# Products of constants ahead of the low-rank and the scaled keys' products in one half of a preparation

## The chip, the cores and the metric

The kernel runs on one core of a Trainium2 chip. A core has five engines with a queue each: TensorE (PE, with its weight loads shown apart as PEld), VectorE (DVE), ScalarE (ACT), GpSimd (POOL) and SyncE (SP, which issues the loads here). The metric is device time in microseconds, the median of several runs. TensorE runs at one of two granted clocks, 2.4 or 1.2 GHz; the profile writes them as 1.00 and 0.50.

## The reference, cut to what matters

One layer over 256 latent tokens with 256 context tokens ahead of them, in float32:

```python
z_x, z_c = split_cols(h_x @ w_in), split_cols(h_c @ w_in)
# RWKV-7 branch, per direction d: context scan, then the latent scan from its final state
wl = w0 + einsum('btzr,zrc->btzc', tanh(lw), w_lora_b)      # low-rank, two directions
decay = exp(-exp(-softplus(-wl) - 0.5))
a = sigmoid(a0 + einsum('btzr,zrc->btzc', la, a_lora_b))
s = s * w_t - (s @ kk_t) (kk_t * a_t)^T + v_t k_t^T         # one step of a scan
# neighbourhood attention beside it, branch merge, output projection
# mixture of 16 experts, top 2, added to the residual
```

## The kernel before, in words

The program is emitted once, straight through, and a list scheduler then orders each engine's queue from dependencies and its own costs; on each queue the order is fixed from then on. Weights come through a ring of three buffers (`wraw`, 512 KB each): a load is issued when the buffer's last user is done.

The scans are done in chunks of 32 tokens. `rw_prep(s, R)` prepares a stream (s = 0 context, s = 1 latent) in two halves f of four heads each, for two directions d: `low_rank(f)` (products into `p2`, `tanh` on ACT, L680), `decays(f, d)` (scan along tokens on DVE, L693; exponentials on ACT, L694 and L695; scaled keys on DVE and POOL, L705 to L710), `products(f, d)` (64 x 64 products of the scaled keys into `pp`, evacuated by DVE, L733, and ACT, L736) and `turn` (transposes). Then `rw_solve` inverts the chunks' triangles on DVE (L785 to L795), and `rw_chain` runs the chunks one after the other. Every matmul is issued at L264 (`mm`), except transposes (L749, L967) and the products of constants (L275).

Between the steps `fill()` pulls steps of a second program, `others()`: projections, attention (`att_core`: logits in `pa`, softmax at L999 to L1005, transposes of the probabilities at L967) and the modulation's rows (`mod_part`, weights `in_modr`, 32 x 256 products into `pb`). In the latent preparation the attention's second group of heads and the modulation stand beside it, and the second half f = 1 begins once the attention is emitted.

`warm(p, site, n)` issues as many products of two constants as the table `WARM` gives for the site, bfloat16, 128 x 128 by n columns, into the PSUM tile p that the products behind it overwrite. Nothing reads them. Each is ordered behind the last matmul of the main program that was emitted before it. Before the change the table has sites in the second half of the latent chain ("x", "y", "z") and behind it ("gn").

Of the kernel before, what the change touches and what calls it, by code (L numbers as in the profile page):

```python
# [168 lines left out]

WARM = {(w, 1, i): n for w, n in (("x", 4), ("y", 3), ("z", 2)) for i in range(3, 8)}  # L170
WARM.update({("gn", i): n for i, n in enumerate((4, 4, 10, 3, 5, 5))})
MIX = [3, 1]
DEEP = [3]

# [58 lines left out]
def hybrid_kernel(ctx: ExitStack, tc: tile.TileContext, a, out, dbg=None, stop=None):  # L233
# [23 lines left out]
    def pb(name="pb"):  # L257
        return ps.tile([128, 512], F32, tag="b", name=name, bufs=4)
# [312 lines left out]
    p, p2 = fout["lw"]  # L571
# [89 lines left out]
    def rw_prep(s, R):  # L661
# [6 lines left out]
        def low_rank(f):  # L668
            for i, (b, src, o) in enumerate(((wlb, lw, 0), (alb, la, 8))):
                p2 = [pb(), pb()]  # L670
                for q in range(2):
                    for d in range(2):
                        r_ = slice(64 * d, 64 * d + 64)
                        Q = 2 * f + q
                        mm(p2[d][:, q * 256:(q + 1) * 256], b[r_, Q * 128:(Q + 1) * 128], src[r_, t_])
                fill()
                for d in range(2):
                    for q in range(2):
                        Q = 2 * f + q
                        S.activation(tmps[d][i][:, q * 256:(q + 1) * 256], p2[d][:, q * 256:(q + 1) * 256], AF.Tanh, scale=0.5,  # L680
                                     bias=hb[:, o + 4 * d + Q:o + 4 * d + Q + 1])
# [31 lines left out]
        def products(f, d):  # L713
            bk, Gd = tmps[d][3], GG[f][d]
            mG = C[f"maskG{d}"]

            w = 32 * nw
            pp = [pb(), pb()]
            for i in range(8):
                if i and i % 2 == 0:  # L720
                    fill()
                for par in range(2):
                    j = 2 * i + par
                    for h in range(2):
                        r_ = slice(64 * h, 64 * h + 64)
                        o_ = 64 - 64 * (h ^ par)
                        mm(pp[par][o_:o_ + 64, i * w:(i + 1) * w], bk[r_, j].rearrange("p w t -> p (w t)"),
                           Gd[r_, h, j // 8, j % 8].rearrange("p w t -> p (w t)"))
            for par in range(2):
                for h in range(2):  # L730
                    ro, o_ = 64 - 64 * h, 64 - 64 * (h ^ par)
                    pv = pp[par][:, 0:8 * w].rearrange("p (c x) -> p c x", x=w)
                    V.tensor_tensor(Gd[ro:ro + 64, h].rearrange("p q c w t -> p (q c) (w t)")[:, par::2], pv[o_:o_ + 64],  # L733
                                    mG[o_:o_ + 64, 0:w].unsqueeze(1).to_broadcast([64, 8, w]), op=ALU.mult)

                    S.activation(NT[ro + 32 * d:ro + 32 * d + 32, :, 2 * f:2 * f + 2].rearrange("p t q c -> p (q c) t")[:, par::2],  # L736
                                 pv[o_ + 32 * d:o_ + 32 * d + 32, :, 0:32], AF.Copy, scale=-1.0)
            tot = 32 if d == 0 else 1
            G.tensor_tensor(bk.ap.rearrange("p c w t -> p c (w t)"), bk.ap.rearrange("p c w t -> p c (w t)"),
                            Es[d][:, :, tot:tot + 1].to_broadcast([128, 16, 64]), op=ALU.mult)  # L740
# [322 lines left out]
    def others():  # L1063
        yield from values()
        done.add("v")
        yield from att_proj(0)
        yield from both_(att_core(0), att_proj(1), MIX[0])
        yield from receptances()
# [167 lines left out]
    for n4 in range(4):  # L1236
        pp = [pa()[:, :256] for _ in range(2)]
# [270 lines left out]
```

## Time and profile before

| | |
|---|---|
| runs, us | 737.54, 741.64, 742.75 (median 741.64) |
| the profiled execution | 737.73 us |
| its span, first to last instruction | 735.9 us |
| mean granted TensorE clock | 0.97 |
| busy share: PE, DVE, ACT, POOL | 93%, 54%, 41%, 14% |

The profile is of one execution. Times in it count from its first instruction. The latent preparation lies at about 255 to 334 us, the latent solve at 334 to 376, the latent chain up to 438, and the experts from 502 on.

### The profile page before, as it was taken

The page shows a single profiled execution, that of the slowest core. Times are in us where ns is not written, and L with a number is a line of the kernel's source. Part 1 is how long each engine was busy: PE and PEld are TensorE (multiplying, and loading weights), DVE is VectorE, ACT ScalarE, POOL GpSimd, SP SyncE. Part 2 cuts the span into 40 slices and gives each one's busy share as a digit, 9 for nine tenths or more (in the row PEclk, how much of TensorE's full clock was granted, in tenths as well). Part 3 has the DMA queues.
Part 4 walks back from the last instruction along what each step waited for, and adds up shares of the span by engine and source line. Part 5 has one row for each costly group of instructions (what it writes and reads, how often), then busy time and mean ns, then how long its engine had stood idle before and what let it go on. Part 6 is the DMA issues. An engine that isn't in the chain of part 4 may idle for free.

```text
span 735.9 us, 14592 instructions
## 1 busy us (share of the span) xinstructions
PE 681.6 (93%) x6053; PEld 455.6 (62%) x6059; DVE 397.4 (54%) x738; ACT 301.4 (41%) x604; POOL 101.0 (14%) x90
## 2 busy tenths in 40 slices
PE   4999788999999979689999998998999999999996
PEld 2667677885777844367988766995534544544532
DVE  2445985999774586968975456844213212212113
ACT  5436677447755366845444423432201101101110
POOL 0002354003223044350012201000000000000000
PEclk9999879999999977999999999999999999999999
DMA  9844011231120343777651158969999999999951
GB/s 363 324 168 134 4 59 37 80 107 59 59 63 20 112 147 113 237 262 261 201 193 60 56 197 306 361 245 381 410 408 411 409 410 412 406 411 411 409 220 61
DMA packets 46297, 165.34 MB, mean 225 GB/s; under 512 B 5392, under 2 KB 6800, under 8 KB 45328
## 3 DMA queue, kind: packets, MB, share of 16 engines
q1 hardware_dynamic: 46224, 164.34, 59.9%
q8 instruction: 49, 0.80, 0.4%
q14 instruction: 24, 0.20, 0.1%
HBM read 163.27 MB, written 1.05 MB: 223 GB/s over the span
## 4 chain that ended last, share of the span: by engine, by line
PE 73%; DVE 12%; ACT 9%; issue 2%; DMA 2%; POOL 1%; DVEq 0%; ACTq 0%; POOLq 0%
PE pa L264 53%; PE pb L264 16%; DVE arena_q L281 3%; ACT arena L753 2%; ACT arena L736 1%; PE pb L275 1%; PE pa L967 1%; ACT arena_q L280 1%; DVE arena L696 1%; DVE arena L790 1%; DVE arena L792 1%; DMA arena<-in_modr_dram 1%; DMA arena<-in_pab_dram 1%; DVE arena L693 1%; PE pb L338 1%
## 5 line engine op out<-in xcount | busy, mean ns | idle before, releaser
L264 PE MATMUL pa<-arena_p,arena_q 128*128 128x256 f32 (+1 forms) x984 | 164.3, 314 | 3.3 <-ACT arena_p L373 1.2
L264 PEld LDWEIGHTS pa<-arena_p,arena_q 128*128 128x128 f32 x984 | 134.5, 189 | 24.1 <-issue 5.5
L264 PE MATMUL pa<-arena,arena_m 128*64 128x512 f32 (+1 forms) x652 | 147.1, 555 | 0.0
L264 PE MATMUL pb<-arena 128*32 128x64 f32 (+13 forms) x2248 | 112.0, 270 | 17.7 <-DVE arena L710 5.7
L264 PEld LDWEIGHTS pb<-arena 128*32 128x32 f32 (+7 forms) x2246 | 70.3, 137 | 54.7 <-issue 19.7
L264 PEld LDWEIGHTS pa<-arena,arena_m 128*64 128x64 f32 x652 | 48.5, 137 | 83.7 <-issue 80.3
L280 ACT CAST arena_q<-arena 128x1024 fp32r<-128x1024 f32 (+1 forms) x66 | 62.8, 955 | 80.9 <-PE pa L264 55.1
L281 DVE TENSOR_TENSOR arena_q<-arena,arena_q 128x1024 fp32r<-128x1024 f32 (+1 forms) x66 | 77.6, 1176 | 23.3 <-ACT arena_q L280 18.7
L1408 DVE TENSOR_TENSOR arena_m<-arena_m,pa 128x512 f32<-128x512 f32 x8 | 5.5, 688 | 96.7 <-PE pa L264 96.7
L264 PE MATMUL pa<-arena_q,arena_p 128*128 128x256 f32 x384 | 57.2, 296 | 0.0
L264 PEld LDWEIGHTS pa<-arena_q,arena_p 128*128 128x128 f32 x384 | 49.4, 194 | 6.3 <-issue 3.6
L813 POOL TENSOR_TENSOR arena<-arena 64x512 f32<-64x512 f32 x30 | 32.0, 1068 | 115.6 <-DVE arena L843 113.7
L1349 ACT ACTIVATE arena_m<-pa,arena 128x128 f32<-128x128 f32 x32 | 12.1, 457 | 78.0 <-PE pa L264 78.0
L264 PE MATMUL pa<-arena_p,arena_m 128*64 128x512 f32 x140 | 41.3, 593 | 0.0
L264 PE MATMUL pa<-arena 128*64 128x256 f32 (+5 forms) x192 | 37.8, 446 | 1.7 <-ACT arena L968 1.7
L280 ACT CAST arena_r<-arena_m 128x512 fp32r<-128x512 f32 x16 | 9.9, 618 | 64.9 <-DVE arena_m L1428 64.9
L1428 DVE SCALAR_TENSOR_TENSOR arena_m<-pa,arena,arena_p 128x512 f32<-128x512 f32 x16 | 12.0, 751 | 43.1 <-PE pa L264 43.1
L264 PEld LDWEIGHTS pa<-arena_m,arena 128*128 128x128 f32 x256 | 30.8, 201 | 6.6 <-issue 5.7
L809 ACT COPY arena<-arena 32x256 f32<-32x256 f32 x64 | 25.8, 403 | 18.7 <-PE pb L264 16.8
L264 PE MATMUL pa<-arena_m,arena 128*128 128x128 f32 x256 | 32.3, 287 | 0.9 <-DVE arena_m L1336 0.9
L843 DVE TENSOR_TENSOR arena<-pb,arena 64x512 f32<-64x512 f32 x30 | 20.7, 689 | 15.9 <-PE pb L264 15.4
L264 PE MATMUL pb<-arena,arena 64*64 64x64 f32 (+1 forms) x496 | 26.9, 251 | 0.7 <-ACT arena L829 0.6
(210 smaller groups left out, 846.2 us busy)
## 6 DMA issues: line engine op xcount, KB each, us to landing
arena<-in_w_dram SPq DMA_DIRECT2D x137, 512.0 KB, 9.6
arena<-in_win_dram SPq DMA_DIRECT2D x42, 512.0 KB, 4.0
arena_p<-in_w_dram SPq DMA_DIRECT2D x35, 512.0 KB, 10.1
arena<-in_modr_dram SPq DMA_DIRECT2D x32, 512.0 KB, 4.1
arena<-in_modw_dram SPq DMA_DIRECT2D x4, 2048.0 KB, 14.3
arena<-in_w_dram SPq DMA_DIRECT2D x20, 256.0 KB, 8.2
arena_m<-in_w_dram SPq DMA_DIRECT2D x10, 512.0 KB, 8.8
arena<-in_pab_dram SPq DMA_DIRECT2D x8, 512.0 KB, 3.2
```

The costliest lines, as they stand in the source:

```text
L264: i = T.matmul(out, lhsT, rhs, start=start, stop=stop, skip_group_check=True)
L275: i = T.matmul(p[:, 512 - n:], cb("ob", 128), cb("scanm", n), start=True, stop=True, skip_group_check=True)
L280: S.copy(dhi.bitcast(F32R), src)
L281: eng.tensor_tensor(dlo.bitcast(F32R), src, dhi, op=ALU.subtract)
L338: T.transpose(p[:, (2 * k + i) * 128:(2 * k + i + 1) * 128], xn[:, 2 * st + i, kc * 128:(kc + 1) * 128], ident)
L693: V.tensor_tensor_scan(cum[:, go], C["scanm"], sg[:, go], 0.0, op0=ALU.mult, op1=ALU.add)
L753: (V.tensor_copy if h and c2 else S.copy)(BT[f][64 - 64 * h:128 - 64 * h, d, q, c2:8:2, :], pv[64 * c2:64 * c2 + 64, :, h, :])
L809: S.copy(Z[rv, h, :, d, :], vt[32 * c4:32 * c4 + 32, h, tt, :, :])
L813: G.tensor_tensor(sd[r_], Z[r_, h], pc[r_, :, :, i].rearrange("p d q -> p q d").unsqueeze(3) .to_broadcast([64, 4, 2, 64]), op=ALU.mult)
L843: V.tensor_tensor(Z1[r_, h], pyv[r_], sd[r_], op=ALU.add)
L1349: S.activation(dst, src, AF.Identity, scale=m4[:, kc:kc + 1], bias=m3[:, kc:kc + 1])
L1428: V.scalar_tensor_tensor(sil.ap, py[n2], gsl[pr % 2].ap, m5r[:, n2 * 512:(n2 + 1) * 512], op0=ALU.mult, op1=ALU.mult)
```

## The change

Two sites are added to the table, each with a call: three products of 512 columns ahead of each of the two parts of `low_rank(0)` of the latent stream, and six of 256 columns ahead of `products(0, d)` for each direction. These are 18 products, 6,144 columns in all. The second half (f = 1) and the context's preparation have none.

```diff
 WARM.update({("gn", i): n for i, n in enumerate((4, 4, 10, 3, 5, 5))})
+WARM.update({("low", 1, 0, i): 3 for i in range(2)})
+WARM.update({("prod", 1, 0, d): 6 for d in range(2)})
...
         def low_rank(f):
             for i, (b, src, o) in enumerate(((wlb, lw, 0), (alb, la, 8))):
                 p2 = [pb(), pb()]
+                warm(p2[i], ("low", s, f, i))
...
             w = 32 * nw
             pp = [pb(), pb()]
+            warm(pp[0], ("prod", s, f, d), 256)
             for i in range(8):
```

The scheduler then orders all queues anew from this place to the solve. Line numbers behind the new lines are larger by 2 to 4 (L264 becomes L266, L275 becomes L277, L693 becomes L696, L705 becomes L708, L999 becomes L1003, L967 becomes L971).

TensorE at the latent low-rank, before: the low-rank products are the rows of 128x256, the attention's logits those of pa 128x512, the modulation's those of 32x256.

```order
L264 MATMUL pb<-arena 128x512 x2
L264 MATMUL pb<-arena 128x256 x6
L264 MATMUL pa<-arena 128x512 x2
L264 MATMUL pb<-arena 128x256 x2
L264 MATMUL pb<-arena 32x256 x8
```

TensorE there, after the change, from the third of the first three products of constants:

```order
L277 MATMUL pb<-arena 128x512
L266 MATMUL pb<-arena 128x256 x4
L277 LDWEIGHTS arena
L277 MATMUL pb<-arena 128x512
L277 LDWEIGHTS arena
L277 MATMUL pb<-arena 128x512
L277 LDWEIGHTS arena
L277 MATMUL pb<-arena 128x512
L266 MATMUL pb<-arena 128x256 x2
L266 MATMUL pa<-arena 128x512
L266 MATMUL pb<-arena 128x256 x2
L266 MATMUL pa<-arena 128x512
```

Six products of constants stand ahead of low-rank products, and the second low-rank part now alternates with the logits.

TensorE ahead of the first `products(0, 0)` (the row of 64x64), before:

```order
L264 MATMUL pa<-arena 128x512 x2
L264 MATMUL pb<-arena 32x256 x4
L967 MATMUL pa<-arena 128x128 x4
L264 MATMUL pb<-arena 32x256 x4
L967 MATMUL pa<-arena 128x128 x4
L264 MATMUL pb<-arena 32x256 x4
L264 MATMUL pa<-arena 128x512
L264 MATMUL pb<-arena 64x64 x32
```

TensorE there, after the change, from the last of the six products of constants:

```order
L277 LDWEIGHTS arena
L277 MATMUL pb<-arena 128x256
L266 MATMUL pb<-arena 32x256 x8
L971 MATMUL pa<-arena 128x128 x4
L266 MATMUL pb<-arena 64x64 x24
L266 MATMUL pb<-arena 32x256 x4
L266 MATMUL pb<-arena 64x64 x8
L266 MATMUL pb<-arena 128x256 x2
L971 MATMUL pa<-arena 128x128 x4
```

The six stand ahead of two units of the modulation and four transposes of probabilities, not directly ahead of the 64x64 products; these have moved ahead of the second four transposes and of two logits.

VectorE at the beginning of `decays(0, 0)`, before (L692, L693, L696, L705 and L707 are the decays, L999 to L1005 the attention's softmax):

```order
L1115 TENSOR_TENSOR arena<-arena,pb 128x512 x2
L999 SCALAR_TENSOR_TENSOR arena<-pa,arena 128x256
L692 TENSOR_SCALAR arena<-arena 128x512 x2
L1002 TENSOR_REDUCE arena<-arena 128x1
L999 SCALAR_TENSOR_TENSOR arena<-pa,arena 128x256
L693 SCALAR_TENSOR_TENSOR arena<-arena 128x512
L696 SCALAR_TENSOR_TENSOR arena<-arena 128x512
L1004 RECIPROCAL arena<-arena 128x1
L1002 TENSOR_REDUCE arena<-arena 128x1
L1005 TENSOR_SCALAR arena<-arena 128x512
L705 TENSOR_TENSOR arena<-arena 64x16x32
L707 TENSOR_TENSOR arena<-arena 64x16x32
```

VectorE there, after the change (L695, L696, L699, L708 and L710 are the decays, L1003 to L1009 the softmax):

```order
L1119 TENSOR_TENSOR arena<-arena,pb 128x512 x2
L695 TENSOR_SCALAR arena<-arena 128x512
L696 SCALAR_TENSOR_TENSOR arena<-arena 128x512
L1003 SCALAR_TENSOR_TENSOR arena<-pa,arena 128x256
L695 TENSOR_SCALAR arena<-arena 128x512
L708 TENSOR_TENSOR arena<-arena 64x16x32
L1006 TENSOR_REDUCE arena<-arena 128x1
L1003 SCALAR_TENSOR_TENSOR arena<-pa,arena 128x256
L699 SCALAR_TENSOR_TENSOR arena<-arena 128x512
L710 TENSOR_TENSOR arena<-arena 64x16x32
L1008 RECIPROCAL arena<-arena 128x1
L1006 TENSOR_REDUCE arena<-arena 128x1
```

The decays' scan has moved ahead of both logits' steps, and the softmax's first normalisation (L1005, now L1009) behind the two scaled keys' steps.

## Rows read from the trace of the kernel before

**Rows 1.** Part 2 of the page: granted TensorE clock, 40 slices of 18.4 us, in tenths.

```profile
PEclk9999879999999977999999999999999999999999
```

**Rows 2.** Windows of 5 us: busy us (instructions) by engine, granted clock, DMA share, GB/s.

```profile
core 0: us, PE busy (x) PEld busy (x) DVE busy (x) ACT busy (x) POOL busy (x), PEclk, DMA share, GB/s
255.00:260.00 5.00, 5.00 (x27) 3.19 (x24) 2.00 (x5) 2.86 (x6) 0.00 (x0) 1.00 0.29 105
260.00:265.00 5.00, 3.03 (x30) 0.88 (x28) 4.89 (x10) 4.46 (x11) 0.99 (x1) 1.00 0.59 207
265.00:270.00 5.00, 2.86 (x16) 1.63 (x16) 5.00 (x8) 2.55 (x6) 3.75 (x4) 0.50 0.53 193
270.00:275.00 5.00, 5.00 (x76) 2.43 (x74) 5.00 (x10) 3.87 (x8) 2.17 (x1) 0.50 0.38 127
275.00:280.00 5.00, 5.00 (x26) 2.26 (x19) 0.46 (x1) 1.54 (x4) 4.94 (x5) 0.50 0.13 36
280.00:285.00 5.00, 5.00 (x23) 2.87 (x23) 4.10 (x8) 2.72 (x6) 0.40 (x1) 0.50 0.35 116
...
295.00:300.00 5.00, 2.66 (x24) 1.63 (x24) 4.53 (x8) 4.80 (x11) 1.28 (x1) 1.00 0.56 193
```

**Rows 3.** Timeline, TensorE, 265 to 287 us: start, length, what, idle before it.

```profile
265.62 1.09 PE L967 MATMUL pa<-arena 128*128 128x128 f32 x4 [2.60 <-DVE arena L1005]
...
269.24 1.09 PE L967 MATMUL pa<-arena 128*128 128x128 f32 x4 [1.52 <-DVE arena L1005]
...
273.27 5.00 PE L264 MATMUL pb<-arena 64*64 64x64 f32 x76
...
280.07 2.92 PE L264 MATMUL pb<-arena 64*128 64x256 f32 x12
...
284.39 2.40 PE L264 MATMUL pb<-arena 64*128 64x256 f32 x28
```

**Rows 4.** Timeline, all engines, 258 to 287 us: the decays, their inputs, their products.

```profile
258.17 1.57 ACT L680 ACTIVATE arena<-pb,arena 128x256 f32<-128x256 f32 x4 [1.87 <-PE pb L264]
...
260.30 0.75 DVE L692 TENSOR_SCALAR arena<-arena 128x512 f32<-128x512 f32 x2
...
261.95 1.21 DVE L693 TENSOR_TENSOR_SCAN arena<-arena 128x512 f32<-128x512 f32 x1
...
264.01 1.18 POOL L705 TENSOR_TENSOR arena<-arena 64x512 f32<-64x512 f32 x1 [25.27 <-ACT arena L694]
...
269.62 0.68 DVE L710 TENSOR_TENSOR arena<-arena 128x512 f32<-128x512 f32 x1
...
272.83 3.02 POOL L705 TENSOR_TENSOR arena<-arena 64x512 f32<-64x512 f32 x1 [4.02 <-ACT arena L694]
...
280.43 0.69 DVE L710 TENSOR_TENSOR arena<-arena 128x512 f32<-128x512 f32 x1 [4.97 <-POOL arena L709]
...
285.99 0.66 PEld L264 LDWEIGHTS pb<-arena 64*64 64x64 f32 x20 [0.33 <-ACT arena L736]
```

**Rows 5.** Groups by line and form, 380 to 450 us: the products of constants there.

```profile
L275 PE MATMUL pb<-arena 128*128 128x256 bf16 x52 | 7.8, 275 | 0.0
L275 PE MATMUL pb<-arena 128*128 128x512 bf16 x24 | 7.5, 381 | 0.8 <-DVE arena L1173 0.5
```

**Rows 6.** Timeline, 300 to 335 us: full clock, a load's wait, the solve's start.

```profile
323.86 0.91 PE L264 MATMUL pb<-arena 64*64 64x64 f32 x32
...
326.70 0.64 PE L264 MATMUL pb<-arena 128*32 128x256 f32 x8 [1.02 <-DMA arena<-in_modr_dram]
...
333.82 1.25 DVE L785 STREAM_TRANSPOSE arena<-arena 128x1024 f32<-128x1024 f32 x1
```

**Rows 7.** Windows by stage, columns as in rows 2: the latent solve, the experts.

```profile
335.00:375.00 40.00, 38.81 (x348) 36.12 (x346) 35.96 (x82) 17.95 (x31) 0.00 (x0) 1.00 0.70 222
...
502.00:706.00 204.00, 203.27 (x1107) 96.22 (x1109) 47.63 (x114) 31.26 (x72) 0.00 (x0) 0.99 1.03 410
```

**Rows 8.** Windows of 5 us in the context's preparation, columns as in rows 2.

```profile
85.00:90.00 5.00, 0.48 (x12) 0.31 (x13) 5.00 (x6) 2.96 (x5) 2.67 (x2) 0.76 0.00 0
```

## The prediction

> **What bounds the kernel now.** Begin with the strip of the granted clock [rows 1]: it falls in two places, slices 5 to 6 (the context's preparation) and slices 15 to 16. The second is the latent preparation, and the windows of 5 us [rows 2] show it: 1.00 up to 265, 0.50 from there to 285, four windows in all. Read TensorE's busy time beside the clock. Before the fall it has 3.03 of 5 us of work, with a hole of 2.60 us that a softmax step ends [rows 3]. In the next window it has 2.86 of 5, and from 270 on it is busy 5.00 of 5, at half speed. VectorE is the opposite: 4.89, 5.00 and 5.00 up to 275, then 0.46 of 5 from 275 to 280. So first TensorE starves behind VectorE, the clock falls, and then everybody waits for a slow TensorE.
>
> What that costs is seen by holding the moment at which an input is ready against the moment at which TensorE reaches it [rows 4]. The last scaled keys of direction 0 are written at 269.62 + 0.68 = 270.30; their products begin at 273.27, since transposes, modulation and logits stand ahead on the queue at half speed. Those of direction 1 are ready at 280.43 + 0.69 = 281.12; their weights are first loaded at 285.99. The price of half speed itself: 64x64 products take 5.00 us for 76 records (66 ns each) against 0.91 for 32 (28 ns) at full clock [rows 3, 6].
>
> What a microsecond here is worth: the solve begins at 333.82 [rows 6] and fills VectorE for 35.96 of 40 us, TensorE for 38.81 [rows 7]. Behind it come the chain and the experts, where the loads run at 1.03 of their share and 410 GB/s for 204 us [rows 7]. Nothing there has slack that waits for a clock time, so I let a shift of the solve's start reach the end in full.
>
> **The change part by part.**
>
> *The products themselves.* By the groups of those that exist [rows 5], 7.5/24 = 0.31 us for 512 columns and 7.8/52 = 0.15 for 256, tails included; by columns at 2.4 GHz, 0.21 and 0.11. So 18 cost between 6 x 0.21 + 12 x 0.11 = 2.6 and 6 x 0.31 + 12 x 0.15 = 3.7 us of TensorE, and the six of direction 1 cost 1.3 instead of 0.65 if the clock is low then. On the path lie the first three, 0.64 to 0.93: they stand directly ahead of the first low-rank products, where TensorE is busy 5.00 of 5 [rows 2], and the first `tanh` at 258.17 [rows 4] waits for those. I take 0.65. The next three delay the second low-rank part as much again, but that is read one scan later. The six ahead of `products(0, 0)` fall into the hole at 263 to 265.6 and cost nothing as long as the hole is there; if the clock is kept and the hole is gone, they cost 0.65.
>
> *The new order of VectorE.* Before, the scan of direction 0 starts at 261.95, though its input step L692 started at 260.30 and takes 0.75 for two [rows 4]; a softmax step and the second L692 stood between. Now it follows directly on its first L692, which waits for two of four `tanh` (half of 1.57) from 258.17 + 0.65: ready at 259.6, scan at about 260.0. That is 1.9 us earlier with the products' delay counted, and the first POOL step of the decays (264.01) moves with it. This gain needs no clock.
>
> *The new order of TensorE.* `products(0, 0)` no longer queue behind the second transposes and two logits. If they start as soon as their input is there, that is 3.0 us earlier than 273.27 even at an unchanged 270.30, and up to 1.9 more with the scan. The other side of this is that the softmax's first normalisation goes behind two scaled keys' steps, so the transposes that ended the hole of 2.60 us come later, not earlier, by about one step of 0.7 to 1.2 us.
>
> *The clock.* The six products put 0.65 us of dense work into a hole of 2.6 us; the hole's end moves out by about the same. What TensorE does around 264 to 269 is then hardly denser than before, so I do not expect the clock to be held through. That much work does not decide it alone is also seen elsewhere: from 295 to 300 TensorE has 2.66 of 5 us and the clock stays at 1.00 [rows 2]; in the context's preparation it has 0.48 of 5 and the clock falls [rows 8]. What I do expect is a later fall, and an earlier return, because the 64x64 products start sooner and six dense products stand directly ahead of those of direction 1.
>
> *The sum.* From the start of `products(0, 0)` to that of direction 1 TensorE works without a hole from 273.27 to 285.99, 12.7 us at half clock. Moved forward by 3.0 and with 1.3 us of products at half clock put in, direction 1 starts at 284.3: a gain of 1.7 at least from the order alone. At full clock the 12.7 become 6.4, and the start is then set by its input: 281.12 less 1.9 for the scan, 279.2, a gain of 6.8. With the low clock over for the second half of that stretch, 284.3 less 3.2 is 281.1, a gain of 4.9. Of this I take off 0.9 for VectorE, which is busy 4.53 of 5 from 295 [rows 2] and passes not all of it on: 4.0 us. The profiled execution, 737.73 (a span of 735.9 and 1.8 around it), would become 733.7. It is the quick one of the runs: their median is 741.64, 3.9 above. I lay the gain to the median and say **737.6 us**.
>
> One rule of the skill speaks against a larger gain. The step that makes direction 1 late is POOL's scaled keys at 272.83, which took 3.02 us where the same step took 1.18 at 264.01 [rows 4]. The Trainium skill, SBUF — State Buffer, "SBUF: two separate sides", says that VectorE and GpSimd share one pair of ports, that whichever starts first holds it for its whole instruction and that the other waits. By that rule no clock of TensorE shortens the 3.02; by the row alone a quieter VectorE could give back 1.8, and the sum would be nearer 731.9. In the new order the same VectorE steps stand beside it, so I keep 3.02.
>
> **The rivals.**
>
> *Held through.* The clock stays at 1.00 in the whole preparation. For it: work from 263 on comes denser, and near a hole of 2.6 us a little may decide. Against it: the hole's end moves out. Direction 1 then starts at 279.2, 6.8 us earlier, and its products and those of the low rank behind it run at 28 ns instead of 66 where they still did not: 6 to 10 us in all, 732 to 735.6.
>
> *Given back by the loads.* The second half is paced not by these steps but by the modulation's weights: at 326.70 TensorE waits 1.02 us for a load [rows 6], and there are three buffers. Then products may start early and the solve still begins near 334. For it: the wait; against it: a load is issued when a product frees its buffer, so loads move with the products, and DMA is busy only 0.13 to 0.38 of the time from 270 to 285 [rows 2]. Time: 740 to 742.5.
>
> *Slower.* One mechanism: the products delay both low-rank parts by 0.65 and 1.3 us, the postponed normalisation widens the hole, the clock falls as before and stays low as long, and the six products of direction 1 cost 1.3 us at half speed on the path. It decides if the low stretch is again 20 us or more and begins no later than about 267. Price: 1.3 + 1.3, plus up to 3 for a softmax chain that ends later and holds the transposes: 744 to 747.
>
> *Not what it says.* The products might stand where TensorE is busy anyhow. The order shows that for the first six of 512 columns: they go into a stretch that was solid. If the six of 256 are also early, only their cost of 2.6 to 3.7 is left, less the order's gain: this ends within the two cases before it.
>
> **How the numbers follow.** Chances: the forecast 0.47 (735.5 to 740), held through 0.25 (731 to 735.5), given back by the loads 0.18, slower 0.10. The runs of before spread over 5.2 us, so each case is as wide again as a run's own noise. The range leaves out 2 in 10: from **731.5** (the lower half of held through lies about there) to **744** (the point where the slower case begins). One per cent of 741.64 is 7.4 us, about what a measurement of this kernel tells from no change: faster than 734.2 takes most of held through and the edge of the forecast, 0.26; slower than 749.1 is only the far end of the last case, 0.04; the rest, 0.70, is within it.
>
> **What would show it.** In the profile of the changed kernel: the scan of direction 0 (now L696) at about 260 instead of 261.95; the first 64x64 products at 269 to 270.5 instead of 273.27; the granted clock falling once, after 266, and back by about 282; the 64x64 products of direction 1 beginning at 279 to 283; the solve's transposition (now L789) at about 329.8. The prediction is wrong if the first 64x64 products are not earlier than 272, if the clock's low stretch is as long as before, or if the solve starts 4 us earlier and the end does not follow.

## The result and the profile after

The changed kernel takes 745.61 us (median of 20 runs, 739.17 to 747.88), the kernel before 738.94 in the same rounds (20 runs, 735.21 to 744.65). The ratio is **1.0062, 95% interval 1.0040 to 1.0083**: by it some 4.6 us slower, by the two medians 6.7. The forecast was 737.6 and faster; 745.61 lies above its range. Ratios leave out executions that lie more than 1.5% above a kernel's quickest.

The strip of the granted clock of the profiled execution after (745.72 us, a span of 743.8), 40 slices of 18.6 us:

```profile
PEclk9999879999999886889999999999999999999999
```

Where the strip of before has one fall from slice 15 on [rows 1], this one is low over slices 14 to 18. Slice 14 is a low stretch of 6.8 us between 235 and 250, ahead of the place of the change. The windows of 5 us, columns as in rows 2, resolve the others:

```profile
260.00:265.00 5.00, 4.95 (x34) 2.60 (x37) 2.90 (x6) 2.75 (x7) 0.00 (x0) 1.00 0.20 81
265.00:270.00 5.00, 3.79 (x42) 1.31 (x34) 4.95 (x9) 4.03 (x11) 4.57 (x4) 1.00 0.64 208
270.00:275.00 5.00, 3.51 (x77) 2.30 (x78) 5.00 (x9) 2.69 (x6) 1.11 (x2) 0.79 0.62 215
275.00:280.00 5.00, 5.00 (x15) 2.83 (x15) 1.97 (x4) 3.14 (x8) 4.94 (x4) 0.50 0.34 105
280.00:285.00 5.00, 3.76 (x10) 0.72 (x9) 2.93 (x6) 1.82 (x4) 1.97 (x2) 0.50 0.30 105
285.00:290.00 5.00, 4.84 (x10) 2.51 (x10) 3.69 (x8) 3.26 (x8) 0.00 (x0) 0.50 0.01 3
290.00:295.00 5.00, 5.00 (x75) 3.05 (x74) 4.29 (x9) 3.40 (x8) 1.48 (x3) 0.66 0.08 15
...
305.00:310.00 5.00, 3.06 (x29) 1.75 (x25) 4.13 (x9) 4.59 (x12) 0.74 (x2) 1.00 0.86 265
310.00:315.00 5.00, 3.61 (x23) 1.49 (x23) 4.14 (x6) 2.88 (x8) 2.03 (x2) 0.55 0.62 227
315.00:320.00 5.00, 5.00 (x20) 2.67 (x19) 1.19 (x3) 1.45 (x3) 2.00 (x2) 0.50 0.41 138
320.00:325.00 5.00, 5.00 (x64) 3.25 (x63) 3.77 (x5) 0.89 (x2) 4.84 (x4) 0.93 0.71 224
```

A window at 0.79 holds (1 - 0.79) x 2 x 5 = 2.1 us at half clock, one at 0.66 holds 3.4. So the first low stretch is 2.1 + 15 + 3.4 = 20.5 us, about as long as before [rows 2]; it only begins later. And there is a **second fall**: 4.5 + 5 + 0.7 = 10.2 us from 310 on, a place where the prediction did not look.

To compare executions whose earlier parts differ (this one is 3.2 us late already when the latent low rank begins), times are counted from here on from the load of the table for the first `tanh`, the last thing that both do alike: 255.02 in the trace of before, 258.20 in that of after. "+18.3" is 18.3 us behind it.

The first half in the timelines of after (start, length, what, idle before it), rows that answer to rows 3 and 4:

```profile
262.00 1.21 ACT L683 ACTIVATE arena<-pb,arena 128x256 f32<-128x256 f32 x3 [2.52 <-PE pb L266]
...
263.34 1.23 DVE L696 TENSOR_TENSOR_SCAN arena<-arena 128x512 f32<-128x512 f32 x1
...
266.75 0.83 PE L277 MATMUL pb<-arena 128*128 128x256 bf16 x6
...
270.95 0.63 PE L971 MATMUL pa<-arena 128*128 128x128 f32 x4 [1.33 <-DVE arena L1009]
272.12 4.59 PE L266 MATMUL pb<-arena 64*64 64x64 f32 x76 [0.54 <-DVE arena L713]
...
274.40 3.02 POOL L708 TENSOR_TENSOR arena<-arena 64x512 f32<-64x512 f32 x1 [3.89 <-ACT arena L697]
...
285.16 5.06 PE L266 MATMUL pb<-arena 64*128 64x256 f32 x10 [1.41 <-ACT arena L683]
290.16 1.46 PE L277 MATMUL pb<-arena 128*128 128x256 bf16 x6
291.55 2.45 PE L266 MATMUL pb<-arena 64*64 64x64 f32 x54
```

Read the starts against those of before: the scan of direction 0 at +5.1 instead of +6.9 [rows 4], `products(0, 0)` at +13.9 instead of +18.3 [rows 3], both earlier as forecast. But `products(0, 1)` begin at +33.4 instead of +31.0 [rows 4]. The products of the second `low_rank` stand ahead of them in both kernels (16 records of 64x256), but after the change the last eight, in the row of 285.16 with two of the modulation, wait for ScalarE's `tanh`, which empties the buffers of PSUM that they write (the pool has four). From the start of `products(0, 0)` to that of `products(0, 1)` 19.4 us pass instead of 12.7.

The second half, from the last softmax steps to the solve. First the kernel before, then the kernel after (L967 and L971 are the transposes of probabilities, `pa` 128*64 the attention's output, L976 and L980 its eviction, L705 and L708 the decays of the second half):

```profile
307.29 0.63 PE L967 MATMUL pa<-arena 128*128 128x128 f32 x4 [2.31 <-DVE arena L1004]
...
309.58 1.94 PE L264 MATMUL pa<-arena 128*64 128x256 f32 x14
...
311.56 0.37 ACT L976 CAST arena_p<-pa 128x256 fp32r<-128x256 f32 x1 [0.16 <-PE pa L264]
...
310.38 1.31 POOL L705 TENSOR_TENSOR arena<-arena 64x512 f32<-64x512 f32 x1 [3.52 <-PE pa L264]
```

```profile
309.57 0.52 PE L971 MATMUL pa<-arena 128*128 128x128 f32 x3 [1.94 <-DVE arena L1009]
...
312.52 0.88 PE L971 MATMUL pa<-arena 128*128 128x128 f32 x3 [1.39 <-DVE arena L1009]
...
316.73 3.67 PE L266 MATMUL pa<-arena 128*64 128x256 f32 x14
...
320.44 0.37 ACT L980 CAST arena_p<-pa 128x256 fp32r<-128x256 f32 x1 [4.00 <-PE pa L266]
...
318.00 1.18 POOL L708 TENSOR_TENSOR arena<-arena 64x512 f32<-64x512 f32 x1 [5.91 <-PE pa L266]
...
342.10 1.25 DVE L789 STREAM_TRANSPOSE arena<-arena 128x1024 f32<-128x1024 f32 x1 [0.32 <-ACT arena L740]
```

After, TensorE waits twice for a softmax normalisation, the clock falls between the two waits, and the same fourteen products take 3.67 us instead of 1.94. The last attention output is evicted at +62.2 instead of +56.5, POOL's decays wait 5.91 us for TensorE, and the solve starts at +83.9 instead of +78.8 [rows 6].

### The profile page after: what moved, and what is told of

Its sections match the earlier page's. It is cut to its first block, busy times and chain, and to the rows that moved or that the text cites. A ratio compares the mean times of both kernels' runs of the same rounds, so it can differ in the third digit from the quotient of the medians.

```text
span 743.8 us, 14636 instructions
## 1 busy us (share of the span) xinstructions
PE 691.5 (93%) x6070; PEld 459.6 (62%) x6077; DVE 395.4 (53%) x738; ACT 301.3 (41%) x604; POOL 100.7 (14%) x90
## 4 chain that ended last, share of the span: by engine, by line
PE 71%; DVE 12%; ACT 8%; DMA 3%; issue 2%; POOL 2%; SPq 0%; DVEq 0%; ACTq 0%; POOLq 0%
PE pa L266 52%; PE pb L266 15%; ACT arena L757 2%; DVE arena_q L283 2%; PE pb L277 2%; DMA arena<-in_win_dram 1%; DVE arena L794 1%; ACT arena L740 1%; DMA arena<-in_w_dram 1%; DVE arena L796 1%; ACT arena_q L282 1%; PE pa L971 1%; DMA arena<-in_x_dram 1%; DVE arena L713 1%; DVE arena L696 1%
## 5 line engine op out<-in xcount | busy, mean ns | idle before, releaser
L266 PE MATMUL pa<-arena_p,arena_q 128*128 128x256 f32 (+1 forms) x984 | 165.3, 316 | 4.7 <-DVE arena_p L377 1.8
L266 PEld LDWEIGHTS pa<-arena_p,arena_q 128*128 128x128 f32 x984 | 135.6, 191 | 25.0 <-issue 5.7
L266 PE MATMUL pa<-arena,arena_m 128*64 128x512 f32 (+1 forms) x652 | 148.8, 561 | 0.0
L266 PE MATMUL pb<-arena 128*32 128x64 f32 (+13 forms) x2248 | 119.0, 273 | 17.9 <-DVE arena L713 6.2
L266 PEld LDWEIGHTS pb<-arena 128*32 128x32 f32 (+7 forms) x2246 | 72.9, 138 | 58.9 <-issue 23.2
L266 PEld LDWEIGHTS pa<-arena,arena_m 128*64 128x64 f32 x652 | 48.8, 138 | 85.1 <-issue 80.0
L266 PE MATMUL pa<-arena_q,arena_p 128*128 128x256 f32 x384 | 58.2, 299 | 0.0
L266 PEld LDWEIGHTS pa<-arena_q,arena_p 128*128 128x128 f32 x384 | 50.3, 197 | 6.3 <-issue 3.6
L266 PE MATMUL pa<-arena_p,arena_m 128*64 128x512 f32 x140 | 41.3, 593 | 0.0
L266 PE MATMUL pa<-arena 128*64 128x256 f32 (+5 forms) x192 | 38.7, 472 | 0.0
L266 PEld LDWEIGHTS pa<-arena_m,arena 128*128 128x128 f32 x256 | 29.2, 192 | 6.6 <-issue 5.7
L266 PE MATMUL pa<-arena_m,arena 128*128 128x128 f32 x256 | 30.7, 278 | 0.9 <-DVE arena_m L1340 0.9
L266 PE MATMUL pb<-arena,arena 64*64 64x64 f32 (+1 forms) x496 | 25.2, 236 | 0.7 <-ACT arena L833 0.6
```

The source lines that it names most:

```text
L266: i = T.matmul(out, lhsT, rhs, start=start, stop=stop, skip_group_check=True)
```

## The experiments

Two theories of the result, and a third that came with the trace: **order** (the scheduler's new order of all queues costs), **work** (the 18 products themselves cost), **clock** (either costs only where it makes the clock fall).

**Order and work apart.** A kernel is built twice. The first build only gives the order of every queue; in the second this order is laid down as order dependences between neighbours of one engine, which are of the kind that adds no semaphore wait, and the products get another size. `order_only` has the changed kernel's order, row for row on all engines, and products of 32 columns; `work_only` has the order of before and full products; `b_dense` and `a_dense` have the order of before and of after and 24 instead of six products ahead of `products(0, 0)` (`b_dense` none at the low rank).

```diff
-WARM.update({("low", 1, 0, i): 3 for i in range(2)})
-WARM.update({("prod", 1, 0, d): 6 for d in range(2)})
+    _counts(3,6,6,512,256)            # low, prod 0, prod 1, columns: gives the order
...
+    _counts(3,6,6,32,32)              # what is run
...
+        for eng, o in orders.items():
+            for x, y in zip(o, o[1:]):
+                tc.add_manual_dep(mine[y], mine[x].name, info, reason="order")
```

Expected of `order_only`:

> Every engine has the changed kernel's order, row for row, but the 18 added products have 32 columns each instead of 512 and 256, so that they cost next to nothing (18 x about 30 ns). If the order is what costs the time (low-rank parts and second scaled keys' products spread behind slots of PSUM, the postponed softmax), the ratio to the kernel before is again 1.006 (about 743.5 us beside 738.9), the first 64x64 products of direction 0 start 4 us earlier and those of direction 1 about 2 us later than before. If the products' own time is what costs, the ratio is 0.995 to 1.000. If TensorE's clock alone decides, the ratio follows the low stretches: 1.000 if there is one of 20 us from about 265, 1.004 to 1.008 if one of 10 us follows it near 310.

Expected of `work_only`:

> All 18 added products at full size, but every other instruction of every engine stands in the order of the kernel before. If the products' own time costs (2.6 to 3.7 us of TensorE, more at half clock), the ratio is 1.003 to 1.006 (741 to 743.5 us). If the order costs, it is 0.998 to 1.002, since at least the first six of 256 columns go in ahead of a hole of 2.6 us. If the clock decides and the dense work ahead of that hole defers the fall, the low stretch is shorter than 20 us and the ratio is 0.992 to 0.998.

Expected of `b_dense`:

> Order of the kernel before; no products at the low rank, 24 of 256 columns (2.6 us at full clock) ahead of the logits and the hole in front of the scaled keys' products of direction 0, and six ahead of those of direction 1. If the clock can be held by dense work there, the granted clock is 1.00 up to at least 275 and direction 1's products start 3 to 6 us earlier than 285.99: ratio 0.992 to 0.996. If the clock falls as before for 20 us, the 24 products only delay: 2.6 us and more on the path, ratio 1.002 to 1.006.

Expected of `a_dense`:

> Order of the changed kernel, with 24 products of 256 columns instead of six in front of direction 0's scaled keys' products. If the order costs, this is at least as slow as the changed kernel: 1.006 to 1.010. If the clock costs and dense work holds it, the low stretch behind 270 is shorter than 15 us and the one near 310 gone: 0.995 to 1.001. If the products' own time costs, it is 2 us more than the changed kernel: 1.008 to 1.010.

Measured: `order_only` 1.0058 (1.0026 to 1.0090), `work_only` 1.0038 (1.0005 to 1.0071), `b_dense` 1.0045 (1.0013 to 1.0077), `a_dense` 1.0103 (1.0053 to 1.0152, 6 runs). The order without the work costs what the whole change costs. Full products in the order of before cost too, by 2.8 us (0.4 at the interval's lower end). Twenty-four dense products did not hold the clock in the first half in either order: in both traces it is low for 17.1 us there, and `a_dense` has the second fall as well, 10.2 us from 308 on.

Why `work_only` is slower is not shown. In its trace the products delay the eight `tanh` of the first half, whose fifth starts at +7.6 instead of +5.8. But it also has a fall of its own, 6.8 us from 298 on, and so has `b_dense`, from 297 on:

```profile
295.00:300.00 5.00, 2.11 (x11) 1.46 (x11) 4.03 (x10) 4.80 (x11) 0.61 (x1) 0.77 0.59 232
300.00:305.00 5.00, 5.00 (x30) 2.67 (x32) 4.97 (x8) 3.98 (x11) 0.66 (x1) 0.55 0.57 197
```

Ten products of an attention output take 2.49 us in this stretch instead of 1.51, and the solve starts at +83.5. TensorE waits 1.67 us before this fall and 1.23 us as it begins. The trace of before has two waits of the same lengths at the same place, and its clock stays at 1.00 [rows 2, 295 to 300]:

```profile
295.95 0.65 PE L264 MATMUL pa<-arena 128*64 128x256 f32 x4 [1.67 <-ACT arena L968]
297.83 1.09 PE L749 MATMUL pb<-arena 128*128 128x128 f32 x8 [1.23 <-ACT arena L736]
```

The windows of `order_only` show the second fall again, 2.3 + 5 + 2.9 = 10.2 us:

```profile
305.00:310.00 5.00, 3.33 (x24) 1.48 (x24) 4.63 (x7) 2.88 (x8) 2.46 (x2) 0.77 0.50 175
310.00:315.00 5.00, 5.00 (x20) 2.86 (x21) 0.80 (x2) 1.94 (x4) 1.50 (x2) 0.50 0.36 102
315.00:320.00 5.00, 5.00 (x43) 3.30 (x40) 4.16 (x5) 0.89 (x2) 4.84 (x3) 0.71 0.58 181
```

Its timeline also shows the wait ahead of `products(0, 1)` without any work of the added products:

```profile
279.49 5.06 PE L267 MATMUL pb<-arena 64*128 64x256 f32 x10 [4.78 <-ACT arena L688]
```

**Which part of the order, and is it the clock?** `a_then_b` has the order of after up to the end of `products(0, 1)` and that of before from there on, `b_then_a` the opposite. `a_hold2` is `order_only` with eight dense products of constants (256 columns) ahead of each of the attention's last four groups of transposes; `b_hold2` puts them into the order of before, without the 18.

```diff
+CUTS = {"DVE": 358, "Activation": 320, "PE": 1743, "SP": 78}
...
+        last[e][:cut] = first[e][:cut]
```

```diff
-        def probs(b, h, L):
+        def probs(b, h, L, n):
             p = pa()
+            warm(p, ("att", g, n), 256)   # 8 each for g = 1, n = 4 to 7
```

Expected of `a_then_b`:

> Every engine has the changed kernel's order up to the end of the scaled keys' products of direction 1 (first half of the latents) and the order of the kernel before from there on; the 18 added products have 32 columns. If the first part of the new order costs, the ratio is again 1.004 to 1.007. If the second part costs (softmax steps and the decays of the second half), it is 0.998 to 1.001, and the solve starts at most 1 us later, counted from the table load of the first tanh (78.8 us in the kernel before, 84.8 with the whole new order). If a second fall of TensorE's clock is what costs, wherever it comes from, the ratio is above 1.003 if the granted clock falls again between 40 and 60 us behind that table load, and within 0.002 of 1 if not.

Expected of `b_then_a`:

> The opposite: order of the kernel before up to the end of direction 1's products, the changed kernel's from there on, added products of 32 columns. If the second part of the new order costs: 1.004 to 1.007, with the last softmax normalisation later by 1 us and the last attention output later by 4 us and more than in the kernel before (52.2 and 56.5 us behind the table load). If the first part costs: 0.998 to 1.001.

Expected of `a_hold2`:

> The changed kernel's whole order with added products of 32 columns, and 8 dense products of 256 columns (0.85 us at full clock) ahead of each of the last four groups of transposes of the attention, where TensorE waits for softmax steps 1.9 and 1.4 us before the clock falls near 310. If that fall costs and dense work averts it, the granted clock stays 1.00 from 40 us behind the table load on, the last attention output comes within 1 us of the kernel before (56.5 us behind the table load) and the ratio is 1.000 to 1.003. If the order costs by itself, 1.005 to 1.008 with the clock up. If the clock falls all the same, up to 3.4 us of dense work come on top: 1.007 to 1.011.

Expected of `b_hold2`:

> Order of the kernel before, none of the 18 products, the same 4 times 8 dense products ahead of the attention's last four groups of transposes. In the profile of before the clock does not fall there, so nothing is to be held: 1.000 to 1.004 by the delay of the products. If the kernel before loses time there in runs that were not profiled, 0.996 to 1.000.

Measured: `a_then_b` 1.0070 (1.0037 to 1.0104, 8 runs), `b_then_a` 1.0043 (1.0017 to 1.0070), `a_hold2` **0.9977** (0.9952 to 1.0003), `b_hold2` 1.0029 (0.9999 to 1.0058). The trace of `b_then_a` has the fall of 10.2 us from 308 on, and its last attention output 4.8 us later than before; that of `a_then_b` has none there, but a first low stretch of 27 us and one of 3.4 us behind 329; without a second fall it was expected within 0.002 of 1. With dense products ahead of the transposes the changed order is 0.8% quicker than without them, although its last attention output still comes at +59.2, later than the expected 57.5; in the order of before the same products, if anything, cost. So the second part's loss goes through the clock. Whether the first part costs by itself is open here.

**Is it the products' density?** `after_hold2` is the changed kernel as it is, all products at full size, with the 32 dense ones; `thin_hold2` is `a_hold2` with 32 columns in these 32; `half_hold2` has four per group. `before_again` profiles the kernel before once more.

```diff
+    _counts(3, 6, 6, 512, 256, {4: 8, 5: 8, 6: 8, 7: 8})      # after_hold2
...
-            warm(p, ("att", g, n), 256)
+            warm(p, ("att", g, n), 32)                         # thin_hold2
...
+    _counts(3, 6, 6, 32, 32, {4: 4, 5: 4, 6: 4, 7: 4})        # half_hold2
```

Expected of `after_hold2`:

> The changed kernel as it is, all 18 products at full size and its own order, with the 4 times 8 dense products of 256 columns ahead of the attention's last four groups of transposes. If the second fall of the clock is what makes the changed kernel slower, it is gone here too and the ratio is 0.997 to 1.001, 4 us below the changed kernel. If the 18 products at full size cost by themselves, 1.002 to 1.005. If the clock falls all the same, 1.007 to 1.010.

Expected of `thin_hold2`:

> The kernel with the changed order that was quicker than before, with the same 32 added products ahead of the last four groups of transposes, but with 32 columns each instead of 256: the same instructions in the same places and hardly any work. If it is the dense work that keeps the clock up, the fall near 310 is back and the ratio is 1.004 to 1.007. If it is only that the instructions stand there (a slot of PSUM taken earlier, the transposes held back a little), the ratio stays at 0.996 to 1.000.

Expected of `half_hold2`:

> The same with four products of 256 columns ahead of each of the four groups instead of eight. If half the work also keeps the clock, it costs up to 1.7 us less than eight where the products stand on the path: 0.994 to 0.998. If it does not keep it, the fall near 310 is back and the ratio is 1.004 to 1.008.

Expected of `before_again`:

> The kernel before, profiled once more: its runs spread over 12 us, and only one has been seen. If a second fall of the clock also comes in some of its executions, this one may show a low stretch between 40 and 60 us behind the first tanh's table load, and then a solve that starts 3 us later than 78.8 us behind it. If its executions differ elsewhere, the latent preparation takes within 1 us of what it took and the difference stands in the context's part or in the experts.

Measured: `after_hold2` 0.9998 (0.9960 to 1.0037), `thin_hold2` 1.0039 (1.0011 to 1.0068), `half_hold2` 1.0003 (0.9970 to 1.0036). The whole loss of the changed kernel is gone with the dense products, and a loss is back with the same instructions and hardly any work. `half_hold2` has no fall there in its trace, but its ratio lies between the two ranges that were expected. Windows of `after_hold2` over the place of the fall, and the one of `thin_hold2` in which its clock falls (columns as in rows 2):

```profile
300.00:305.00 5.00, 5.00 (x54) 3.95 (x47) 4.45 (x9) 4.06 (x11) 2.03 (x3) 1.00 0.83 288
305.00:310.00 5.00, 4.82 (x40) 2.91 (x38) 3.62 (x6) 3.48 (x7) 1.44 (x2) 1.00 0.54 179
310.00:315.00 5.00, 5.00 (x68) 3.20 (x64) 3.77 (x5) 0.89 (x2) 4.84 (x4) 1.00 0.83 265
```

```profile
305.00:310.00 5.00, 3.71 (x17) 1.60 (x18) 3.00 (x6) 3.14 (x7) 0.95 (x1) 0.66 0.52 171
```

This execution of `thin_hold2` is its second quickest (738.18 us, the median is 741.60): its fall lasts 3.4 us only and is over before the fourteen products of the attention's output, which take 1.94 us; the solve starts at +81.8.

`before_again` took 742.50 us, 4.8 more than the execution in rows 1 to 8. Its strip has no fall near 310 either:

```profile
PEclk9999969999999977999999999999999999999999
```

Its table load lies 1.6 us later (256.62; from 85 to 125, in the context's preparation, the granted clock is 0.74 instead of 0.83). Its solve begins at +80.3 instead of +78.8: a wait of 2.49 us for a load of the modulation ends at 329.6, and the clock is low for 3.4 us from 331 on. From the solve's start to the end it takes 1.6 us more. So these 4.8 us of the kernel before's own spread are not the fall near 310, and two traces are compared from a common point, not from their start.

**Which rows bring the fall.** `middle_a` has the order of before everywhere but in one stretch, which stands as in the changed kernel: 24 rows of TensorE, 26 of VectorE, 26 of ScalarE, the attention's last softmax steps, transposes and modulation units. `middle_b` is the opposite: the changed kernel's order with this stretch as before. `b_then_a_hold2` adds the dense products to `b_then_a`; `a_then_b2` is `a_then_b` once more.

```diff
+CUTS = {'DVE': (358, 384), 'Activation': (320, 346), 'PE': (1743, 1767)}
...
+        last[e][x:y] = inner[e][x:y]
```

Expected of `middle_a`:

> The order of the kernel before on every engine, but for one stretch: 26 instructions of VectorE, 26 of ScalarE and 24 products or transposes of TensorE, from the end of direction 1's scaled keys' products of the first half to the last scaled keys of the second (the attention's last softmax steps, transposes and modulation units), stand in the changed kernel's order. Added products of 32 columns. If these rows bring the second fall, the granted clock falls for about 10 us some 50 us behind the first tanh's table load, and the ratio is 1.003 to 1.006. If the fall comes from what stands ahead of or behind them, there is none and the ratio is 0.999 to 1.002.

Expected of `middle_b`:

> The opposite: the changed kernel's order everywhere but in this stretch, which stands as in the kernel before. If these rows bring the second fall, it is gone: 0.998 to 1.002, and the last attention output comes within 1.5 us of 56.5 us behind the table load. If not, the fall is there and the ratio is 1.004 to 1.007.

Expected of `b_then_a_hold2`:

> Order of the kernel before up to the end of direction 1's products, the changed kernel's behind it (1.0043 without more), and 4 times 8 dense products of 256 columns ahead of the attention's last four groups of transposes. If the second part costs only through the fall, the fall is gone and the ratio is 0.997 to 1.001. If its order costs too, 1.002 to 1.005.

Expected of `a_then_b2`:

> The kernel with the changed order in the first part alone, once more (1.007 with an interval of 1.0037 to 1.0104 on 8 runs, where its profiled execution was 2.7 us behind the profiled execution of before). If the first part costs by itself, again above 1.004. If it does not, 0.998 to 1.003, and then a low stretch of the clock of some 17 to 20 us from 268 instead of 27.

Measured: `middle_a` **1.0077** (1.0042 to 1.0113), `middle_b` **0.9952** (0.9925 to 0.9979), `b_then_a_hold2` 0.9966 (0.9937 to 0.9995), `a_then_b2` 1.0011 (0.9978 to 1.0044). These 76 rows bring the whole loss into the order of before, and the changed order without them is quicker than both kernels. TensorE's rows at that place, before (the transposes are L967, a unit of the modulation is 32x256 x4):

```
235 L264 MATMUL pb<-arena 32x256 x4
236 L967 MATMUL pa<-arena 128x128 x4
237 L264 MATMUL pb<-arena 32x256 x4
238 L967 MATMUL pa<-arena 128x128 x4
239 L264 MATMUL pb<-arena 32x256 x4
240 L967 MATMUL pa<-arena 128x128 x4
241 L264 MATMUL pb<-arena 128x4 x2
242 L967 MATMUL pa<-arena 128x128 x4
```

and after (transposes L971):

```
276 L266 MATMUL pb<-arena 32x256 x4
277 L971 MATMUL pa<-arena 128x128 x11
278 L266 MATMUL pb<-arena 32x256 x4
279 L971 MATMUL pa<-arena 128x128 x4
280 L266 MATMUL pb<-arena 32x256 x4
281 L971 MATMUL pa<-arena 128x128
```

Before, a unit of the modulation stands between two groups of transposes and is done while VectorE makes the next probabilities; after, three groups follow each other. TensorE's timeline in `middle_a` (where the transposes are L976, as in `middle_b`):

```profile
308.03 0.52 PE L976 MATMUL pa<-arena 128*128 128x128 f32 x3 [1.45 <-DVE arena L1014]
...
310.98 0.88 PE L976 MATMUL pa<-arena 128*128 128x128 f32 x3 [1.60 <-DVE arena L1014]
...
315.62 3.68 PE L267 MATMUL pa<-arena 128*64 128x256 f32 x14
```

and in `middle_b`, where the waits come elsewhere and the attention's output runs at full clock:

```profile
304.51 0.64 PE L267 MATMUL pb<-arena 128*32 128x256 f32 x8 [1.42 <-DMA arena<-in_modr_dram]
...
306.74 0.63 PE L976 MATMUL pa<-arena 128*128 128x128 f32 x4 [0.36 <-DVE arena L1013]
...
308.13 2.68 PE L267 MATMUL pa<-arena 128*64 128x256 f32 x16
```

**One engine's rows, and the whole change on the order of `middle_b`.** `mid_pe` exchanges TensorE's 24 rows alone; `after_mid` is `middle_b` with the 18 products at full size.

```diff
-CUTS = {'DVE': (358, 384), 'Activation': (320, 346), 'PE': (1743, 1767)}
+CUTS = {'PE': (1743, 1767)}                                   # mid_pe
...
+    _counts(3, 6, 6, 512, 256)                                # after_mid
```

Expected of `after_mid`:

> The changed kernel with its 18 products at full size and its order everywhere but in the stretch of the attention's last softmax steps, transposes and modulation units, which stands as in the kernel before. With products of 32 columns this gave 0.9952. If the products cost their own 0.7 to 2 us, 0.996 to 0.999; if they hold the clock in the first half, 0.990 to 0.995; if the fall comes back, above 1.003.

Expected of `mid_pe`:

> The changed kernel's order on every engine, but for TensorE's 24 rows in that stretch, which stand as in the kernel before: each group of four transposes followed by a modulation unit. Added products of 32 columns. If TensorE's own order makes the holes (no other work between the groups of transposes), the fall near 310 is gone and the ratio is 0.995 to 1.000. If VectorE's and ScalarE's order of softmax steps makes them, the fall stays and the ratio is 1.003 to 1.007.

Measured: `after_mid` 0.9961 (0.9921 to 1.0000), while the medians of all its executions and of before's are equal (742.2 both); its profiled execution, 744.63 us, has a fall of 6.8 us from 313 on. `mid_pe` 0.9988 (0.9955 to 1.0021), and its profiled execution has the fall of 10.2 us from 307 on, with other waits ahead of it:

```profile
305.35 0.64 PE L267 MATMUL pb<-arena 128*32 128x256 f32 x8 [2.72 <-DMA arena<-in_modr_dram]
...
310.40 1.01 PE L267 MATMUL pb<-arena 128*128 128x4 f32 x4 [1.95 <-ACT arena L632]
...
312.30 4.42 PE L267 MATMUL pa<-arena 128*64 128x256 f32 x16
```

In this trace of `mid_pe` the solve starts at +85.4, as late as with the whole new order; that its 741.87 us is still no more than the median of before goes with a granted clock of 0.99 over its first 250 us, against 0.97 in rows 1 to 8. Both kernels are inconclusive: one profiled execution with the fall does not say how many of the others have it. What the products cost at full size on the order of `middle_b`, and whether TensorE's rows alone make the difference, stays open.

Some milestones side by side, in us behind the table load, each the start of the instruction in the timeline of its trace less the start of the table load there:

| | before | after | order_only | after_hold2 | middle_a | middle_b |
|---|---|---|---|---|---|---|
| first `tanh` | 3.2 | 3.8 | 3.2 | 3.8 | 3.2 | 3.2 |
| scan, direction 0 | 6.9 | 5.1 | 4.6 | 5.1 | 8.2 | 4.6 |
| first eviction of `products(0, 1)` | 38.6 | 37.9 | 38.7 | 37.4 | 40.2 | 38.7 |
| scan of the second half, direction 0 | 33.9 | 34.3 | 33.7 | 34.2 | 35.5 | 33.7 |
| last softmax normalisation | 52.2 | 53.1 | 53.6 | 52.6 | 54.1 | 53.4 |
| last attention output evicted | 56.5 | 62.2 | 62.8 | 58.1 | 63.7 | 57.8 |
| solve starts | 78.8 | 83.9 | 84.8 | 79.2 | 85.8 | 80.0 |

At the scan of the second half the columns lie within 2 us of each other. The last normalisation is 0.3 to 1.9 us later than before in all of them; between it and the eviction of the output 4.3 to 5.5 us pass at full clock and 9.1 to 9.6 where it falls.

## Why the prediction was wrong, by its own steps

- **The products' cost held.** The first `tanh` is 0.65 us later (+3.80 against +3.15), the term taken. The six of direction 0 took 0.83 us, the six of direction 1, at half clock, 1.46 (forecast 1.3).
- **VectorE's new order held.** The scan is at +5.1; forecast 260.0, which is +5.0.
- **`products(0, 0)` held.** +13.9; forecast 269 to 270.5, which is +14.0 to +15.5. POOL's step takes 3.02 us as before, as taken.
- **The clock failed.** The step was "a later fall, and an earlier return". The fall is later (+14.7 instead of +10.0), the return too: the stretch is 20.5 us again. In `a_hold2` it is 30.7 us, in `after_hold2` 3.4 and 10.2; none of the variants kept it up.
- **"Direction 1 starts at 284.3: a gain of 1.7 at least from the order alone" failed.** It was worked out by moving a solid stretch of 12.7 us forward as a block, with 1.3 us put in. The stretch takes 19.4 us: in the new order the last of the second `low_rank` in that block wait for `tanh`, 1.41 us in the trace of after, 4.78 in `order_only`. `products(0, 1)` begin 2.4 us later; their first eviction is 0.7 us earlier than before (+37.9 against +38.6), but no gain is left when the second half's scan begins (+34.3 against +33.9).
- **The step that decides: the gain was carried from the first half to the solve less 0.9 us**, as if the rest were unchanged. The order of the rest was not read, though the scheduler orders all queues anew up to the solve. There lie the 76 rows that let the clock fall a second time, and in the trace of after the solve starts 5.1 us later (+83.9 against +78.8) where 4.0 earlier was forecast. `middle_b`, which puts them back, is quicker than before by 0.48%; that is the size of the forecast gain (737.6 of 741.64 is 0.54%), without the 18 products' own work and with an interval of 0.2 to 0.75%, so not proof that its working was right.
- **Two readings were off without deciding the result.** The 66 ns for a 64x64 product at half clock came from a row [rows 3] that also holds twelve wider products. The 64 small ones take 2.0 us by themselves, 31 ns each, against 28 at full clock, so "held through" put too much on them, and so did the halving of 12.7 to 6.4. And the 731.9 of a quicker POOL step is counted from the profiled execution's 733.7; from the 737.6 of the forecast it would be 735.8.
- **The rival "slower"** had the time, 744 to 747, and one of its parts, a softmax chain that holds the transposes; its place and its condition were wrong (a first stretch of 20 us that begins before 267; it began at 273). It had 0.10, and the range ended where it began.
- **The rival "given back by the loads"** did not come: the longest wait for a load of the modulation in this part of the trace after is 0.83 us.

That a fall of the clock is the cause is shown: by dense work that removes it and the loss (1.0062 to 0.9998, 1.0058 to 0.9977, 1.0043 to 0.9966), by the same instructions without the work (1.0039), and by the order of before with the 76 rows alone (1.0077).

The traces agree among themselves: in the seven that have a fall of 6.8 us or more from about +52 to +55 on, the solve starts at +82.5 to +85.8; in the ten whose clock does not fall between +42 and +65 it starts at +78.2 to +80.8, and in the three with a shorter or an earlier fall (`thin_hold2`, `work_only`, `b_dense`) at +80.0 to +83.5. The mean granted clock over the executions behind each ratio points the same way. It is 0.959 in `order_only` against 0.968 in the kernel before beside it, 0.961 against 0.968 in `b_then_a`, 0.960 against 0.966 in `middle_a` and 0.960 against 0.969 in `thin_hold2`; where the loss is gone it is 0.972 against 0.969 (`after_hold2`), 0.969 against 0.966 (`b_then_a_hold2`) and 0.966 against 0.966 (`middle_b`). `a_hold2` is the exception, with 0.965 against 0.968 and no loss.

Not settled: whether the new order of the first part costs by itself. The same kernel gave 1.0070 and 1.0011, with a mean clock of 0.960 against 0.968 the first time and 0.965 against 0.966 the second. Also open is which engine's rows in the stretch count, what the 18 products cost by their own work (`work_only`), and why the clock falls in some executions and not in others.

## What to carry to other kernels

Where a scheduler orders the queues, a small edit is a new order everywhere behind it: compare the whole order up to the next point where all engines meet, and look in it for groups of one engine that wait for the same producer and have lost the work that stood between them. Test order and work apart, by laying down the one order and running the other's work. A TensorE that waits twice for 1.4 to 1.9 us in a row can cost more than these waits, where the clock falls with them and what follows on the path runs at half speed.

## What the runs showed of the hardware

- Between two waits of 1.94 and 1.39 us, with 3.06 of 5 us of work in the window ahead, the granted clock fell to half and stayed there for 10.2 us; with 4.82 and 5.00 of 5 us of work at the same place it stayed at 1.00. Neither figure decides it alone: the kernel before has 2.71 of 5 us at that place, with a wait of 2.31 us, and stays at 1.00:

```profile
305.00:310.00 5.00, 2.71 (x19) 1.98 (x21) 4.68 (x10) 3.93 (x11) 1.81 (x2) 1.00 0.80 248
```

- Two waits of 1.67 and 1.23 us close behind each other left the clock at 1.00 in the trace of before; in `work_only`, with waits of the same lengths, 6.8 us at half clock began in the second.
- The Trainium skill, TensorE: Matmul & The Clock Gate, "HAM oscillation — how this bites in real kernels", describes products too short to cover the wait for the next input, and a clock that falls in each wait. The trace of after agrees in that the clock falls at short work between waits, with waits for VectorE instead of a load; it does not agree in "each", by the two rows of the kernel before named here.
- The 32 dense products, work that nothing reads, made the changed kernel 0.6% quicker (1.0062 to 0.9998); in the order of before, in whose traces the clock does not fall there, the ratio with the same 32 is 1.0029 (0.9999 to 1.0058).
- The fall is not certain: two kernels whose ratio is not above 1 (`mid_pe`, `after_mid`) have it in the one execution that was profiled.
